# Two-block transformer kernel: one PSUM layout throughout, three plain indices per feed-forward layer, the second layer's parameters ordered late

## The chip, the cores and the metric

The kernel runs on one core of a Trainium2 chip. The metric is the device time of one execution in microseconds, the median of several runs. The engines are TensorE (PE, matmuls, with its weight loads shown as PEld), VectorE (DVE), ScalarE (ACT), GpSimd (POOL) and SyncE (SP), which issues all DMAs. Each engine has one queue of instructions and runs it strictly in order.

## The reference

Two transformer blocks follow each other, each with two layers, on 512 tokens of width 1024. The first puts 16 learned tokens in front (T = 528) and has in each layer a mixer (differential attention beside a gated recurrence) and a SwiGLU feed-forward part of inner width 2816. The change touches only this first block, above all the feed-forward part:

```python
for l in range(DEPTH):                      # DEPTH = 2
    hn = rms_norm(h, norm_mix_g[l])
    ...                                     # attention and recurrence, added to h
    hn = rms_norm(h, norm_ffn_g[l])
    g, u = jnp.split(hn @ w_gu[l], [D_FF], axis=-1)
    h = h + (jax.nn.silu(g) * u) @ w_down[l]
return h[:, N_META:, :]
```

The second block (convolution, two attentions, cross attention, squared-ReLU network) takes h as its input and is left as it is.

## The kernel before

All of it is float32. A product of two matrices is made of three matmuls with inputs that are split into a high and a low part (mm3, L105 to 108): the high part is a cast on ACT, the low part a subtraction on DVE, written by weight (L100, L102) for weights and by split (L200, L201) for the rest. The tensors stand with the feature on the partitions, in tiles of 128, and the tokens along the columns. Layer 0 computes all 528 columns in halves of 264, layer 1 only the 512 that are kept, in halves of 256.

**The feed-forward part** (FFN0 in layer 0, FFN1 in layer 1) goes through 22 indices; an index is one tile of 128 gate rows and one of 128 up rows (weight tiles t = 2i and 2i + 1). The first two indices are plain: early (L663 to 674) multiplies each weight tile with the normed input, 8 products of 128x128 on each half of the columns (24 matmuls a half), applies silu on ACT for a gate tile (L674) and multiplies with the up tile on DVE (L672). The input itself comes into being in that stretch, piece by piece (L682 to 696).

All other indices go through seven (L170 to 197), a scheme that makes the 2x2 block product out of seven block products (84 matmuls instead of 96). It needs sums of weight blocks: halves4 (L146 to 168) loads two weight tiles (wraw, wraw2) and lets POOL form ws (two operations, L155 and L156), a difference in place (L157) and ws4 (L158); then each is split on ACT and DVE. The results of the seven products (p1 to p7) are combined by DVE in a tile called quarters, after ACT has copied p1 to u (L186). ACT's silu (sl, L722) and POOL's gate product (L723) follow, and ACT and DVE split the result into yh and yl (L200, L201).

**The down projection** follows in five groups of 5, 5, 4, 4 and 4 indices (L728 to 744). A group has 8 tiles m of output rows; both halves of the columns stand in a pair of banks, and one DVE addition of all columns puts them into the residual h (hall, L743). Before a group starts, one index more than it needs is made, so seven-product indices come in runs of 4 (two plain ones ahead of them), 5, 4, 4 and 3.

**PSUM** has 8 banks. In the mixers and in block 2 they are handed out singly: three to mm, two to sc, one each to tr, av and bc. For a feed-forward part the pool is closed and another opened in which three pairs of banks (two) replace mm and sc; bank hands out the halves of a pair one after the other, so that the two parts of a pair are released together.

**What sets the order.** The program is written as loops; a scheduler turns it into one fixed list for each engine, by priorities that follow the order of writing. A buffer count (bufs) says how many tiles of one name may live at once; the next one waits until the last reader of the oldest is done. tc.issue_after puts what is made inside its scope behind a given instruction in the list. The small parameters of a layer (lt, gs and lc, L371 to 402, nearly all on DVE with 1 to 8 columns) depend on one DMA alone, so the scheduler puts those of layer 1 wherever it finds room.

## Time and profile before

| what | value |
|---|---|
| runs | 2880.06, 2882.56, 2883.85 us, median 2882.56 |
| the profiled execution | 2885.76 us, its span 2883.9 us, mean granted clock 0.982 |
| busy in the span | PE 2761.7 us (96%), DVE 1926.9 (67%), ACT 1323.9 (46%), POOL 719.8 (25%) |
| stages, us from the start | mixer 0 to 279, FFN0 to 665, mixer 1 to 909, FFN1 to 1288, block 2 to 2884 |

TensorE's clock as granted has two levels, 1.2 and 2.4 GHz, written as 0.5 and 1.0. In a table of busy times each stretch has the busy microseconds of each engine, with the number of instructions in brackets. In rows by time the first number is the start, the second the duration in us; what stands in square brackets is the time for which the engine idled before it and what released it. A name before the arrow is written, names behind it are read; the DVE pipeline lets the next instruction start a little before the last one's end.

### The profile page before, as it was taken

Reading aid. Unit: us, or ns where it says so; the run is one execution under the profiler, and the core shown is the slowest. Engines: PE = TensorE matmul, PEld = TensorE weight load, DVE = VectorE, ACT = ScalarE, POOL = GpSimd, SP = SyncE. Lnnn points to the kernel's source line nnn. Section 1 sums busy time; section 2 is a strip of 40 time slices with the busy share of each in tenths; the row PEclk is TensorE's granted clock in tenths of the full one; section 3 lists DMA queues with packets and bytes.
Section 4 is the critical chain, followed back from the end, with each engine's and each line's share of the span. In section 5 each row is a group of like instructions: output and inputs, shape, how many; then the busy total and the mean of one; then the engine's idle time right before and its main releaser. Section 6 shows DMA issues by size and latency. Waiting matters only on the chain.

```text
span 2883.9 us, 46217 instructions
## 1 busy us (share of the span) xinstructions
PE 2761.7 (96%) x17652; PEld 2467.3 (86%) x17652; DVE 1926.9 (67%) x3710; ACT 1323.9 (46%) x2366; POOL 719.8 (25%) x637
## 2 busy tenths in 40 slices
PE   8988899999998899999999999999999999999998
PEld 7888899999876899997789888888877898888887
DVE  7887866668888766668987563333689875633335
ACT  6664433436664433344675443332345754433323
POOL 0011644530112454433211031111322010311112
PEclk9999899999999999999999999999999999999999
DMA  4332133323332233335524213333255242133232
GB/s 146 88 79 92 47 102 94 99 78 119 87 82 84 73 101 100 104 97 142 144 74 134 72 59 108 96 95 95 76 140 145 67 134 79 59 102 95 95 96 66
DMA packets 101117, 277.41 MB, mean 96 GB/s; under 512 B 13856, under 2 KB 20512, under 8 KB 100896
## 3 DMA queue, kind: packets, MB, share of 16 engines
q1 hardware_dynamic: 100896, 274.45, 31.6%
q8 instruction: 140, 2.29, 0.3%
q14 instruction: 81, 0.66, 0.1%
HBM read 241.82 MB, written 2.10 MB: 85 GB/s over the span
## 4 chain that ended last, share of the span: by engine, by line
PE 78%; DVE 12%; issue 3%; POOL 3%; ACT 2%; DMA 1%; ACTq 0%; DVEq 0%; POOLq 0%; SPq 0%
PE mm L107 16%; PE mm L108 16%; PE mm L106 16%; PE two L108 6%; PE two L106 6%; PE two L107 6%; PE av L106 1%; PE av L107 1%; PE av L108 1%; DVE wlo L102 1%; PE av L240 1%; DVE wlo L201 1%; DVE sq L481 1%; PE av L851 1%; PE bc L966 1%
## 5 line engine op out<-in xcount | busy, mean ns | idle before, releaser
L100 ACT CAST whi<-wraw 128x1024 fp32r<-128x1024 f32 (+2 forms) x412 | 386.2, 941 | 627.5 <-PE mm L107 504.8
L106 PE MATMUL mm<-xh_all,whi 128*128 128x512 f32 (+2 forms) x1696 | 590.8, 351 | 15.0 <-ACT xh_all L339 7.1
L102 DVE TENSOR_TENSOR wlo<-wraw,whi 128x1024 fp32r<-128x1024 f32 (+2 forms) x389 | 458.2, 1179 | 209.5 <-ACT whi L100 208.4
L107 PE MATMUL mm<-xl_all,whi 128*128 128x512 f32 (+2 forms) x1696 | 593.9, 351 | 1.6 <-DVE xl_all L884 1.0
L108 PE MATMUL mm<-xh_all,wlo 128*128 128x512 f32 (+2 forms) x1696 | 590.0, 349 | 0.0
L106 PEld LDWEIGHTS mm<-xh_all,whi 128*128 128x128 f32 x1696 | 323.7, 192 | 53.2 <-ACT xh_all L339 7.1
L107 PEld LDWEIGHTS mm<-xl_all,whi 128*128 128x128 f32 x1696 | 324.4, 191 | 38.4 <-DVE xl_all L884 2.2
L108 PEld LDWEIGHTS mm<-xh_all,wlo 128*128 128x128 f32 x1696 | 325.3, 192 | 34.6
L1245 POOL TENSOR_TENSOR r<-r 128x512 f32<-128x512 f32 (+1 forms) x70 | 101.9, 1455 | 533.2 <-ACT r L1244 533.2
L106 PE MATMUL two<-yh,whi 128*128 128x264 f32 (+1 forms) x704 | 198.8, 283 | 1.8 <-ACT yh L200 1.8
L108 PE MATMUL two<-yh,wlo 128*128 128x264 f32 (+1 forms) x704 | 198.8, 283 | 0.0
L107 PE MATMUL two<-yl,whi 128*128 128x264 f32 (+1 forms) x704 | 198.4, 282 | 0.0
L106 PE MATMUL two<-xh_all,whi 128*128 128x264 f32 (+1 forms) x448 | 133.5, 301 | 18.4 <-DVE quarters L672 11.8
L812 DVE TENSOR_TENSOR hall<-hall,mm 128x512 f32<-128x512 f32 (+1 forms) x82 | 46.5, 567 | 146.0 <-PE mm L108 146.0
L107 PE MATMUL two<-xl_all,whi 128*128 128x264 f32 (+1 forms) x448 | 134.1, 300 | 4.1 <-DVE xl_all L689 4.1
L107 PE MATMUL two<-tl,whi 128*128 128x264 f32 (+1 forms) x480 | 136.2, 284 | 0.0
L108 PE MATMUL two<-th,wlo 128*128 128x264 f32 (+1 forms) x480 | 136.1, 283 | 0.0
L106 PE MATMUL two<-th,whi 128*128 128x264 f32 (+1 forms) x480 | 135.9, 283 | 0.0
L108 PE MATMUL two<-xh_all,wlo 128*128 128x264 f32 (+1 forms) x448 | 132.7, 297 | 2.2 <-DVE wlo L102 1.2
L106 PEld LDWEIGHTS two<-yh,whi 128*128 128x128 f32 x704 | 132.5, 188 | 2.2 <-ACT yh L200 2.2
L201 DVE TENSOR_TENSOR wlo<-wraw,whi 128x1024 fp32r<-128x1024 f32 x80 | 119.7, 1496 | 21.2 <-ACT whi L200 20.8
L107 PEld LDWEIGHTS two<-yl,whi 128*128 128x128 f32 x704 | 132.4, 188 | 0.1
(724 smaller groups left out, 7480.1 us busy)
## 6 DMA issues: line engine op xcount, KB each, us to landing
wraw<-w2f SPq DMA_DIRECT2D x128, 512.0 KB, 3.8
wraw<-w1gu SPq DMA_DIRECT2D x88, 512.0 KB, 3.6
wraw<-w2in SPq DMA_DIRECT2D x44, 512.0 KB, 3.8
wraw<-w1in SPq DMA_DIRECT2D x40, 512.0 KB, 3.6
wraw<-w2mkv SPq DMA_DIRECT2D x32, 512.0 KB, 3.6
wraw<-w1dn SPq DMA_DIRECT2D x48, 256.0 KB, 2.7
wraw<-w1dn SPq DMA_DIRECT2D x32, 320.0 KB, 2.9
wraw<-w1out SPq DMA_DIRECT2D x32, 256.0 KB, 2.7
```

Of the source, the lines that this page charges most:

```text
L100: nc.scalar.copy(hi[:, :kt], raw[:, :kt])
L102: (eng or nc.vector).tensor_sub(lo[:, :kt], raw[:, :kt], f(hi[:, :kt]))
L106: nc.tensor.matmul(ps, wh, xh, start=first, stop=False)
L107: nc.tensor.matmul(ps, wh, xl, start=False, stop=False)
L108: nc.tensor.matmul(ps, wl, xh, start=False, stop=last)
L201: nc.vector.tensor_sub(lo, x, f(hi))
L240: nc.tensor.matmul(ps[:ch, 2 * j:2 * j + 2], x[:, a + ch * j:a + ch * j + ch], rhs[:, :2], start=e == 0, stop=e == len(xs) - 1)
L481: nc.vector.tensor_mul(sq[:, a0:b0], sq[:, a0:b0], sin1[:, a0:b0])
L812: nc.vector.tensor_add(X(m, a, b), X(m, a, b), p)
L851: nc.tensor.matmul(ps[:, 4 * n + 2 * j:4 * n + 2 * j + 2], x[:, o:o + 128], one2, start=e == 0, stop=e == 1)
L966: nc.tensor.transpose(ps[:, 128 * j:128 * j + 128], p[:, 128 * j:128 * j + 128], ident)
L1245: nc.gpsimd.tensor_mul(r[:, a:b], r[:, a:b], r[:, a:b])
```

## The change

- One PSUM pool with the single banks stays open all the time. The pairs, and the closing and reopening around each feed-forward part, are gone.
- seven takes seven single banks, in the order tr, mm, sc, mm, sc, mm, sc for p1, p2, p6, p5, p7, p3, p4, and has seven DVE additions of one half of the columns.
- Three indices of each layer are plain instead of two (weight tiles t = 0 to 5), and quarters has three buffers in both layers.
- ws in halves4 has one buffer instead of two.
- The down projection uses proj: in layer 0 two halves with an addition each, in layer 1 one matmul of 512 columns for each weight, and one addition.
- The parameters of layer 1 are issued behind the addition for tile m = 0 of layer 0's last group.

```diff
-    def open_psum(name):
-        nonlocal psum, banks, paired, halves
-        paired, halves = name == "psum_f", None
-        banks.close()
-        banks = ExitStack()
-        psum = banks.enter_context(tc.tile_pool(name=name, bufs=1, space=bass.MemoryType.PSUM))
-
-    open_psum("psum")
+    psum = ctx.enter_context(tc.tile_pool(name="psum", bufs=1, space=bass.MemoryType.PSUM))
     EARLY = 4
     BANKS = {"mm": 3, "sc": 2, "tr": 1, "av": 1, "bc": 1}
...
-        s = pool.tile([128, 8, 128], F32, name="ws", bufs=2)
+        s = pool.tile([128, 8, 128], F32, name="ws", bufs=1)
...
-        p1 = bank("av")[:, :n]
-        p26, p57, p34 = (pair_of_banks()[:, :, :n] for _ in range(3))
+        p1, p2, p6, p5, p7, p3, p4 = (bank(t)[:, :n] for t in ("tr", "mm", "sc", "mm", "sc", "mm", "sc"))
         product(p1, a11, b11)
         nc.scalar.copy(u, p1)
-        product(p26[:, 0], a12, b21)
-        product(p26[:, 1], s2, t2)
-        nc.vector.tensor_add(e[:, 0:4:3], p26, twice(u))
-        product(p57[:, 0], s1, t1)
-        product(p57[:, 1], s3, t3)
-        nc.vector.tensor_add(e[:, 1:3], p57, twice(e[:, 3]))
-        nc.vector.tensor_add(e[:, 3], p57[:, 0], e[:, 2])
-        product(p34[:, 0], s4, b22)
-        product(p34[:, 1], a22, t4)
-        nc.vector.tensor_add(e[:, 1:3], p34, e[:, 1:3])
+        product(p2, a12, b21)
+        nc.vector.tensor_add(e[:, 0], p2, u)
+        product(p6, s2, t2)
+        nc.vector.tensor_add(e[:, 3], p6, u)
+        product(p5, s1, t1)
+        nc.vector.tensor_add(e[:, 1], p5, e[:, 3])
+        product(p7, s3, t3)
+        nc.vector.tensor_add(e[:, 2], p7, e[:, 3])
+        nc.vector.tensor_add(e[:, 3], p5, e[:, 2])
+        product(p3, s4, b22)
+        nc.vector.tensor_add(e[:, 1], p3, e[:, 1])
+        product(p4, a22, t4)
+        nc.vector.tensor_add(e[:, 2], p4, e[:, 2])
...
+            with ExitStack() as order:
+                if ended is not None:
+                    order.enter_context(tc.issue_after(ended.ins))
+
+                lt = small.tile([128, 8], F32)
...
-                firsts = [ff.tile([128, 4, half], F32, name="quarters", bufs=2 if l else 3) for _ in range(2)]
+                firsts = [ff.tile([128, 4, half], F32, name="quarters", bufs=3) for _ in range(3)]
...
-                    for t, n, j in ((0, n0, 0), (1, n0, 0), (2, n0, 0), (0, n1, 1), (1, n1, 1), (2, n1, 1), (3, n0, 0), (3, n1, 1)):
+                    for t, n, j in ((0, n0, 0), (1, n0, 0), (2, n0, 0), (0, n1, 1), (1, n1, 1), (2, n1, 1), *((t, n, j) for t in (3, 4, 5) for n, j in ((n0, 0), (n1, 1)))):
...
-                    if i < 2:
+                    if i < 3:
...
-                        e = seven(ff, w, rhs, half, 2 if l else 3)
+                        e = seven(ff, w, rhs, half, 3)
...
-                        ps = pair_of_banks()[:, :, :half]
-                        for j, n in enumerate((n0, n1)):
-                            for k, (yh, yl) in enumerate(ys):
-                                mm3(ps[:, j], w[0][:, k], w[1][:, k], yh[:, n], yl[:, n], k == 0, k == nf - 1)
-                        t = h[m][:, l0:].rearrange("p (a b) -> p a b", a=2)
-                        nc.vector.tensor_add(t, t, ps)
+                        for p, a, b in proj(w, ys, late):
+                            done = nc.vector.tensor_add(h[m][:, a:b], h[m][:, a:b], p)
+                            if f0 + nf == 22 and m == 0:
+                                ended = done
```

How the instructions stand on an engine follows from the scheduler, so three places are shown as they stand in its lists. Line numbers of the changed kernel are 8 to 24 lower: L651 is the former L672, L177 the former L201, L718 the former L743.

DVE at the front of FFN0, before: the last splits of the input (tl), then layer 1's parameters ahead of the product of a plain index.

```order
L201 TENSOR_TENSOR tl<-tt_3702,th 128x792
L371 TENSOR_TENSOR lt<-par 128x1
L372 TENSOR_TENSOR lt<-par 128x1
L381 TENSOR_SCALAR gs<-par 128x1
L382 TENSOR_SCALAR gs<-par 128x1
L383 TENSOR_SCALAR gs<-par 128x8
```

The same place after:

```order
L177 TENSOR_TENSOR tl<-tt_3699,th 128x792
L92 TENSOR_TENSOR wlo<-wraw,whi 128x1024
L651 TENSOR_TENSOR quarters<-quarters,mm 128x264
L92 TENSOR_TENSOR wlo<-wraw,whi 128x1024 x2
L651 TENSOR_TENSOR quarters<-quarters,mm 128x264
```

The product follows after one weight split; before, fifteen parameter operations stood between the two.

DVE at the end of FFN0, after: the additions of the last group, with the parameters between them; before, only additions, weight splits and the next norm's rows stood here.

```order
L718 TENSOR_TENSOR hall<-hall,mm 128x264 x2
L92 TENSOR_TENSOR wlo<-wraw,whi 128x512
L351 TENSOR_TENSOR lt<-par 128x1
L352 TENSOR_TENSOR lt<-par 128x1
L361 TENSOR_SCALAR gs<-par 128x1
L362 TENSOR_SCALAR gs<-par 128x1
L718 TENSOR_TENSOR hall<-hall,mm 128x264
L317 SCALAR_TENSOR_TENSOR xl_all<-hall,par,xh_all 128x528
```

Of the parameter operations 25 stand ahead of the last addition to the norm's sum (ss_acc).

ACT between two seven-product indices, before: silu of the finished one, the copy u of the next one's p1, then the cast yh of the finished one.

```order
L200 CAST whi_5193<-wraw2_5177 128x1024
L722 ACTIVATE sl_5168<-quarters_5073 128x528
L186 COPY u1_5202<-av_5203 128x264
L200 CAST yh2_5171<-quarters_5073 128x528
L200 CAST whi_5313<-wraw_5303 128x1024
```

The same place after:

```order
L701 ACTIVATE sl_5213<-quarters_5112 128x528
L176 CAST whi_5238<-wraw2_5222 128x1024
L176 CAST yh2_5216<-quarters_5112 128x528
L159 COPY u1_5247<-tr_5248 128x264
L176 CAST whi_5364<-wraw_5354 128x1024
```

The copy u and the cast yh have changed places, and the second weight's cast has come between silu and yh.

## Rows read from the trace of the kernel before

**Rows 1.** Window, length; busy (x) PE, PEld, DVE, ACT, POOL; PEclk, DMA share, GB/s

```profile
318.00:640.00 322.00, 321.82 (x2619) 321.39 (x2620) 222.47 (x271) 125.76 (x178) 150.04 (x92) 0.99 0.31 93
957.00:1265.00 308.00, 306.12 (x2560) 305.51 (x2559) 208.99 (x252) 125.01 (x178) 148.53 (x91) 0.99 0.31 94
```

**Rows 2.** TensorE's waits, FFN0 front (total us, times, longest).

```profile
PE two L106 <- DVE quarters L672: 8.0, 1, 8.0
```

**Rows 3.** TensorE's waits, FFN1 front.

```profile
PE two L106 <- DVE quarters L672: 3.8, 1, 3.8
...
PE two L106 <- ACT whi L100: 2.1, 1, 2.1
...
PE two L108 <- DVE wlo L102: 1.2, 1, 1.2
```

**Rows 4.** DVE in order of time, FFN0 front: start, duration, line, what.

```profile
309.72 1.22 DVE L371 TENSOR_TENSOR lt<-par 128x1 f32<-128x1 f32 x1
310.86 0.15 DVE L372 TENSOR_TENSOR lt<-par 128x1 f32<-128x1 f32 x1
...
317.58 0.43 DVE L672 TENSOR_TENSOR quarters<-quarters,two 128x264 f32<-128x264 f32 x1
```

**Rows 5.** Busy table in steps of 5 us, both fronts.

```profile
316.00:321.00 5.00, 2.94 (x13) 2.94 (x14) 4.79 (x12) 0.00 (x0) 1.04 (x1) 0.50 0.11 12
321.00:326.00 5.00, 5.00 (x35) 5.00 (x34) 3.56 (x8) 1.34 (x2) 1.28 (x1) 0.79 0.61 201
...
943.00:948.00 5.00, 5.00 (x24) 4.72 (x24) 1.32 (x3) 1.57 (x2) 5.00 (x4) 0.53 0.28 101
...
953.00:958.00 5.00, 2.39 (x11) 2.40 (x12) 4.18 (x8) 0.83 (x3) 0.00 (x0) 0.66 0.00 0
958.00:963.00 5.00, 5.00 (x32) 5.00 (x32) 3.10 (x7) 3.39 (x6) 0.00 (x0) 0.66 0.07 13
```

**Rows 6.** TensorE in order of time: 256 columns in FFN1, 512 in block 2.

```profile
1099.79 0.28 PE L107 MATMUL two<-yl,whi 128*128 128x256 f32 x1
...
1101.91 0.28 PE L107 MATMUL two<-yl,whi 128*128 128x256 f32 x1
...
1797.72 0.39 PE L106 MATMUL mm<-y0h,whi 128*128 128x512 f32 x1
...
1802.94 0.39 PE L108 MATMUL mm<-y7h,wlo 128*128 128x512 f32 x1
```

**Rows 7.** POOL in order of time, FFN0, weights of an index.

```profile
336.31 1.28 POOL L155 TENSOR_TENSOR ws<-wraw 128x512 f32<-128x512 f32 x1 [13.34 <-DMA wraw<-w1gu]
337.67 2.17 POOL L156 TENSOR_TENSOR ws<-ws,wraw 128x512 f32<-128x512 f32 x1
...
343.75 1.32 POOL L723 TENSOR_TENSOR quarters<-quarters,sl 128x528 f32<-128x528 f32 x1
346.30 1.34 POOL L155 TENSOR_TENSOR ws<-wraw 128x512 f32<-128x512 f32 x1 [1.23 <-DMA wraw<-w1gu]
```

**Rows 8.** DVE in order of time, same place.

```profile
345.77 0.71 DVE L201 TENSOR_TENSOR yl<-quarters,yh 128x528 fp32r<-128x528 f32 x1 [3.13 <-ACT yh L200]
...
349.26 1.70 DVE L201 TENSOR_TENSOR wlo<-ws,whi 128x1024 fp32r<-128x1024 f32 x1
...
358.02 1.23 DVE L201 TENSOR_TENSOR wlo<-wraw,whi 128x1024 fp32r<-128x1024 f32 x1 [0.24 <-ACT whi L200]
```

**Rows 9.** ACT in order of time, the cast behind the gate product.

```profile
414.58 0.63 ACT L200 CAST yh<-quarters 128x528 fp32r<-128x528 f32 x1 [2.69 <-POOL quarters L723]
```

**Rows 10.** DVE and TensorE, layer change, last addition to the norm's sum.

```profile
668.63 0.70 DVE L265 TENSOR_TENSOR ss_acc<-ss_acc,ss_sq 128x528 f32<-128x528 f32 x1
...
669.51 0.64 PE L240 MATMUL av<-one,ss_acc 128*88 128x2 f32 x7
```

**Rows 11.** TensorE, end of FFN1.

```profile
1289.03 0.36 PE L106 MATMUL mm<-xh_all,whi 128*128 128x256 f32 x1 [0.87 <-DVE hall L743]
```

More of the change, by code (lines that the diff above doesn't have):

```diff
@@ L108, in mm3 @@
         nc.tensor.matmul(ps, wl, xh, start=False, stop=last)
-    halves = None
     def bank(name):
-        nonlocal halves
-        if name == "mm" and paired:
-            if halves is None:
-                got = psum.tile([128, 2, 512], F32, name="two", bufs=3)
-                halves = got[:, 1]
-                return got[:, 0]
-            got, halves = halves, None
-            return got
         n = turns[name] = turns.get(name, 0) + 1
@@ L138, in proj @@
         return got
-    def twice(p):
-        return p[:, None, :].to_broadcast([128, 2, p.shape[1]])
-    def pair_of_banks():
-        return psum.tile([128, 2, 512], F32, name="two", bufs=3)
     def halves4(pool, w1, w2):
@@ L367, in both_blocks @@
                 nc.scalar.copy(rbc[:, a:b], p)
-            lt = small.tile([128, 8], F32)
-            nc.vector.tensor_mul(lt[:, 0:1], col(LAM), col(LAM + 1))
-            nc.vector.tensor_mul(lt[:, 1:2], col(LAM + 2), col(LAM + 3))
-            ps = bank("av")
-            nc.tensor.matmul(ps[:, :2], ones, lt[:, 0:2], start=True, stop=True)
-            nc.scalar.activation(lt[:, 2:4], ps[:, :2], AF.Exp, scale=float(D))
-            nc.vector.tensor_sub(lt[:, 4:5], lt[:, 3:4], lt[:, 2:3])
-            nc.vector.tensor_scalar(lt[:, 5:6], lt[:, 4:5], -lam_init, None, op0=OP.add)
@@ L398, in both_blocks @@
-            nc.vector.tensor_mul(lc[:, 4], lc[:, 4], lc[:, 2])
-            nc.vector.tensor_scalar(lc[:, 5], L, 0.0, None, op0=OP.min)
-            nc.vector.scalar_tensor_tensor(lc[:, 6], lc[:, 4], -2.0, lc[:, 5], op0=OP.mult, op1=OP.add)
-            nc.vector.tensor_scalar(lc[:, 7], lc[:, 6], 2.0, None, op0=OP.mult)
-            nc.vector.tensor_scalar(lc[:, 8], lc[:, 6], 4.0, None, op0=OP.mult)
+            with ExitStack() as order:
+                if ended is not None:
+                    order.enter_context(tc.issue_after(ended.ins))
+                lt = small.tile([128, 8], F32)
+                nc.vector.tensor_mul(lt[:, 0:1], col(LAM), col(LAM + 1))
+                nc.vector.tensor_mul(lt[:, 1:2], col(LAM + 2), col(LAM + 3))
+                ps = bank("av")
+                nc.tensor.matmul(ps[:, :2], ones, lt[:, 0:2], start=True, stop=True)
+                nc.scalar.activation(lt[:, 2:4], ps[:, :2], AF.Exp, scale=float(D))
+                nc.vector.tensor_sub(lt[:, 4:5], lt[:, 3:4], lt[:, 2:3])
+                nc.vector.tensor_scalar(lt[:, 5:6], lt[:, 4:5], -lam_init, None, op0=OP.add)
+                neglam = lt[:, 5:6]
+                gs = small.tile([128, 10], F32)
+                nc.vector.tensor_scalar(gs[:, 0:1], col(QG), 0.125, None, op0=OP.mult)
+                nc.vector.tensor_scalar(gs[:, 1:2], col(SUB), 1.0 - lam_init, None, op0=OP.mult)
+                nc.vector.tensor_scalar(gs[:, 2:10], par[:, BRG:BRG + 8], 0.5, None, op0=OP.mult)
+                lc = small.tile([128, 9, 4], F32)
+                L = par[:, LRU:LRU + 4]
+                nc.scalar.activation(lc[:, 0], L, AF.Abs)
+                nc.scalar.activation(lc[:, 1], lc[:, 0], AF.Exp, scale=-1.0)
+                nc.vector.tensor_scalar(lc[:, 2], lc[:, 1], 2.0, None, op0=OP.add)
+                nc.vector.reciprocal(lc[:, 2], lc[:, 2])
+                nc.vector.tensor_mul(lc[:, 2], lc[:, 2], lc[:, 1])
+                nc.vector.tensor_mul(lc[:, 3], lc[:, 2], lc[:, 2])
+                nc.vector.memset(lc[:, 4], 1.0 / 17.0)
+                for n in (15, 13, 11, 9, 7, 5, 3, 1):
+                    nc.vector.tensor_mul(lc[:, 4], lc[:, 4], lc[:, 3])
+                    nc.vector.tensor_scalar(lc[:, 4], lc[:, 4], 1.0 / n, None, op0=OP.add)
+                nc.vector.tensor_mul(lc[:, 4], lc[:, 4], lc[:, 2])
+                nc.vector.tensor_scalar(lc[:, 5], L, 0.0, None, op0=OP.min)
+                nc.vector.scalar_tensor_tensor(lc[:, 6], lc[:, 4], -2.0, lc[:, 5], op0=OP.mult, op1=OP.add)
+                nc.vector.tensor_scalar(lc[:, 7], lc[:, 6], 2.0, None, op0=OP.mult)
+                nc.vector.tensor_scalar(lc[:, 8], lc[:, 6], 4.0, None, op0=OP.mult)
@@ L775, in phase @@
             close(range(nm - tail, nm), w, xs, evac)
-    with banks, blk2:
+    with blk2:
         def parts(pool, name, shape=None, **kw):
```

32 lines of the change are left out of this document (7 added, 25 removed).

## The prediction

> **What bounds the kernel now.** I read the busy table by stage first, then the list of what TensorE waited for in each stage, then the rows around each long wait. In the first block's two feed-forward stages (FFN0 and FFN1) TensorE is the bound once the seven-product indices run: 321.82 us busy of 322, and 306.12 of 308 [rows 1]. A matmul of 264 columns takes 0.122 us there (321.82 us for 2619 recorded ones is 0.123, and a few records are missing). So a matmul saved is time gained and a new wait is time lost. Ahead of those stretches stands the costliest part. In FFN0 TensorE waits 8.0 us once, for the DVE product of a plain index at L672 [rows 2]. The rows show why: DVE ran the next layer's small parameter operations from 309.72 on, first of them 1.22 us long though it has one column, and reached L672 only at 317.58 [rows 4]. In FFN1 the same place waits 3.8 us, after two waits of 2.1 and 1.2 us for a weight's two casts [rows 3]. Behind each long wait the clock stands at its lower level for some microseconds: 35 matmuls in 5 us at a mean grant of 0.79, or 24 at 0.53 [rows 5], between the levels of 1.2 and 2.4 GHz.
>
> **The change, part by part.** Sums are against the profiled run, 2885.8 us (span 2883.9); the median of the runs shown is 3.2 us lower, and I carry the sum over to it.
>
> *The front of FFN0.* Gone is the 8.0 us wait, and for two reasons: the parameter operations leave this stretch, and the second half of the third weight tile no longer shares a pair of banks with the product that is late. The lower clock behind it goes too: 35 matmuls stand in 321 to 326 where 5 us hold 41, 0.7 us, and 13 ahead of them took 2.94 us instead of 1.6, 1.3 us [rows 5]. A third plain index takes 96 matmuls where a seven-product index takes 84: 12 x 0.122 = 1.5 us more. Together -8.6 us. Following the changed order through the stage row by row gives -9.2; I take -9, bounds -5 and -10.
>
> *The front of FFN1.* The 3.8 us go, with 11 matmuls in 2.39 us (1.1 lost) and 32 instead of 42 behind them (1.2 lost) [rows 5]. The 2.1 us wait is filled by the freed second half (24 matmuls, 2.8 us); the weight behind it is then about 1.4 us late, in place of the 2.1 and 1.2. Of what the lower clock took behind those two (24 matmuls where 42 fit, 2.2) I count 2.0 as gained. Against that stand 12 x 0.118 = 1.4 us of matmuls: 3.8 + 2.3 + 1.9 + 2.0 - 1.4 = 8.6. The row by row walk gives 9.7; I take -9, bounds -4 and -10, since DVE's margin at the sixth tile is under half a microsecond.
>
> *Down projection of layer 1.* 1056 matmuls of 256 columns become 528 of 512. Starts lie 0.118 and 0.227 us apart (18 steps in 2.12 us, 23 in 5.22) [rows 6]: 1056 x 0.118 - 528 x 0.227 = 124.6 - 119.9, so -4.7 us; I take -5. The Trainium skill (TensorE: Matmul & The Clock Gate, Back-to-back issue gap) gives N/2.4 ns and 2.5 ns on top; worked out, 109 and 216 ns, that would be an estimate of 1.4 us instead of 4.7, and the rows, being of this kernel, decide.
>
> *Parameters ordered late.* Thirty-one small DVE operations move to the end of FFN0. In the layer change the last addition into the norm's sum starts at 668.63 and TensorE takes it at 669.51 without a wait [rows 10], so DVE time added there is on the path. With POOL quiet such an operation takes 0.15 us [rows 4] and frees DVE in about half of that: some 25 ahead of the sum, 1.9 to 3.7 us; two additions of 264 for one of 528 (2 x 0.35 against 0.62, durations less the 0.08 us by which the next one overlaps) over seven tiles, 0.5 us; less a 1.15 us weight operation that now comes behind the sum, and about 1 us of gaps that absorb some. Net +2, bounds 0 and +5. At the end of FFN1 the 0.87 us that the pool switch costs [rows 11] may go: -0.5, bounds -0.9 and 0.
>
> *Seven products on single banks, one ws buffer.* For seven additions of one half, 0.43 us each like the product at L672 [rows 4], DVE has room: it is busy 222 us of 322 [rows 1]. The buffer is the part that costs. So far POOL's first addition (L155) starts the next index's weights as soon as the DMA lands: 346.30, while DVE is still to read the previous sum, 349.26 to 350.96 [rows 7, 8]. With one buffer it must wait for that read. Behind it on POOL stand three more additions and the gate product (L723), in order. Behind that product stand ACT's cast yh, and behind yh, in the changed order, ACT's copy of the next index's first product u, which so far went ahead of it; on DVE yl stands ahead of the additions that need u, and the next read of ws stands behind those. This is a closed loop, and I add it up.
> POOL's five operations took 336.31 to 345.07, 8.8 us [rows 7], the slow ones because each takes turns with a wide DVE operation; undisturbed they are 1.28 to 1.32 each, 6.4 us. With two instead of four DVE operations beside them: 7.7. Then yh 0.63, yl 0.71 [rows 8, 9] with u and the next cast beside it, the first addition 0.35, the low part of the first weight 1.23 (its cast adds 0.3), two additions 0.8, the read of ws 1.23: 5.1 with the hand-overs, as a wide operation frees DVE a little before its end. The loop takes 12.8 us for an index. TensorE needs 84 x 0.122 = 10.25, in layer 1 9.9. It notices at the last product, the third on the two sc banks: it must have the bank that DVE's second addition, inside the loop, gives back.
> So a seven-product index in the middle of a run loses 2.6 us (layer 1: 2.9). Runs are short, since the down projections between them let POOL catch up: per layer runs of 3, 5, 4, 4 and 3. Going through each run, its second index loses 0.6 to 1.9, the middle ones the full amount, the first and the last nothing. FFN0: 1.3 + (0.6 + 2.6 + 2.6) + 2 x (0.6 + 2.6) + 0.6 = 14.1. FFN1: 1.9 + (0.9 + 2.9 + 2.9) + (0.9 + 2.9) + (1.6 + 2.9) + 1.6 = 18.5, less the 1.9 us that this stretch waits already (308 less 306.12). In the down projections of FFN0 the three single banks and two additions for a tile cost another 2.0. Together +33. Bounds: with POOL undisturbed the loop is 11.5, and the losses are half, +17; with the 8.8 of the rows it is 13.9 and they are +43.
> Behind waits of 2.6 to 2.9 us the clock may fall as it does behind 3.8. Of eight such waits, two are followed by another wait that swallows the loss. I take +3, bounds 0 and +14.
>
> **Sum:** -9 - 9 - 5 + 2 - 0.5 + 33 + 3 = +14.5 us, 2900 for a run like the profiled one; on the median of 2882.6 it is **2897 us**.
>
> **The rivals.**
> *POOL is in time (faster).* If the gate product runs as soon as it may, u and the additions come in time and neither the buffer nor the queue behind it costs more than 5 us. It decides at the gate product: started within about 2.5 us of the end of the silu before it, the second addition still ends before the last product wants the bank, 6 x 1.46 = 8.8 us into the index. For it speaks that POOL's first additions so far start long before they are needed [rows 7]; against it that even undisturbed operations make the loop 11.5 where 10.25 is wanted. -21.5 + 5 = -16.5, so 2866.
> *The buffer costs nothing, the queue still does (no change).* Then u still stands behind yh and the gate product behind three additions, and the walk through the rows leaves about half the losses, +17 of 33: -4.5, so 2878, and up to 2888 with some clock lost.
> *The clock falls behind each wait (slower still).* The 3.8 us wait was followed by 2.3 us lost to the lower level [rows 5]; six of the eight long waits at that price make 14 instead of 3: 2908. The Trainium skill (TensorE: Matmul & The Clock Gate, A second HAM failure mode: psum-queue depth-cycling) says that turning through banks can make TensorE pause so often that its clock goes back and forth between its levels. No row here shows that yet: the two stretches stand at 0.99 [rows 1].
> *The change does not do what it says.* The order shows that the parameter operations do leave the front, so this could only be a front that waits as long for something else: 9 to 18 us of the gain are missing, and it ends near 2910.
>
> **How the numbers follow.** Forecast 0.50 (2888 to 2905), clock or front worse 0.20 (2905 to 2918), buffer free but queue not 0.17, POOL in time 0.13. The range that holds eight in ten leaves out most of the last and the end of the second: 2873 to 2916. A measurement of this kernel tells about 0.2%, 5.8 us, from no change, so faster is under 2876.8 and slower over 2888.3: faster 0.15, which takes in the lower end of the third case, the same 0.17, slower 0.68.
>
> **What the profile of the changed kernel would show.** Right: no wait of more than 2 us before the first seven-product index; in the middle of each run TensorE waiting 2 to 3 us before the last product, released by the second addition; POOL's first addition waiting for DVE's read of ws and not for a DMA; 12 to 13 us from one read of ws to the next; 512-wide matmuls 0.227 us apart; a wait of about 2 us at the first norm of layer 1. Wrong: seven-product indices 10.25 us apart throughout, or POOL still waiting for DMAs. The prediction falls if the loop takes under 11 us, or if the sc bank is given back before the last product needs it.

## The result, and the profile after

The changed kernel takes 2904.88 us, median of four runs (2902.96 to 2907.69), beside 2883.2 for the kernel before (one run more than in the table above): a ratio of 1.0077, 95% interval 1.006 to 1.0095, so 22 us slower. The forecast was 2897, slower, with 2873 to 2916 as its range. The profiled execution took 2905.03 us with a span of 2903.2, 19.3 more than before, where the sum had 14.5; the rest of the 22 us is that the profiled execution of before lay above its median.

The stages, each from TensorE's matmul on the norm's sum to the last matmul of the down projection, say where it went. FFN0 took 396.8 us instead of 385.2, FFN1 390.5 instead of 378.6; mixer 1 and block 2, which the change touches only at their starts, were 1.9 and 1.2 us shorter, the first mixer 1.2.

Busy times of the seven-product stretches after, in the columns of [rows 1]:

```profile
330.00:645.00 315.00, 299.93 (x2413) 297.21 (x2412) 208.33 (x320) 116.33 (x164) 130.49 (x87) 0.99 0.30 88
966.00:1270.00 304.00, 287.25 (x1930) 265.41 (x1930) 197.21 (x278) 111.81 (x160) 130.34 (x88) 0.98 0.31 90
```

TensorE had been busy for all but 0.2 and 1.9 us of such a stretch [rows 1]; now 15 and 17 us are idle. What it waited for, in FFN0 and then in FFN1 (total us, times, longest):

```profile
PE sc L96 <- DVE quarters L163: 13.6, 9, 2.5
PE mm L96 <- ACT yh L176: 1.4, 1, 1.4
PE mm L96 <- DVE hall L718: 1.3, 2, 0.7
...
PE sc L96 <- DVE quarters L163: 18.0, 9, 2.8
PE mm L96 <- ACT yh L176: 0.5, 1, 0.5
```

Nearly all of it is one wait: the last product p4 wants an sc bank (L96), and DVE's second addition (L163) has not given it back. The loop behind it can be read in one index in the middle of FFN0's run of five. Rows by time, POOL first, then ACT, DVE and TensorE:

```profile
413.12 1.29 POOL L129 TENSOR_TENSOR ws<-wraw 128x512 f32<-128x512 f32 x1 [5.30 <-DVE wlo L177]
...
419.55 1.32 POOL L702 TENSOR_TENSOR quarters<-quarters,sl 128x528 f32<-128x528 f32 x1
...
426.17 1.28 POOL L129 TENSOR_TENSOR ws<-wraw 128x512 f32<-128x512 f32 x1 [5.29 <-DVE wlo L177]
...
420.91 0.63 ACT L176 CAST yh<-quarters 128x528 fp32r<-128x528 f32 x1 [5.09 <-POOL quarters L702]
421.44 0.37 ACT L159 COPY u<-tr 128x264 f32<-128x264 f32 x1
...
421.57 0.71 DVE L177 TENSOR_TENSOR yl<-quarters,yh 128x528 fp32r<-128x528 f32 x1 [4.38 <-ACT yh L176]
422.20 0.43 DVE L161 TENSOR_TENSOR quarters<-mm,u 128x264 f32<-128x264 f32 x1
...
423.94 0.43 DVE L163 TENSOR_TENSOR quarters<-sc,u 128x264 f32<-128x264 f32 x1
...
424.82 1.22 DVE L177 TENSOR_TENSOR wlo<-ws,whi 128x1024 fp32r<-128x1024 f32 x1
...
424.42 0.59 PE L96 MATMUL sc<-th,whi 128*128 128x264 f32 x1 [2.54 <-DVE quarters L163]
424.81 0.42 PE L97 MATMUL sc<-tl,whi 128*128 128x264 f32 x1
425.02 0.42 PE L98 MATMUL sc<-th,wlo 128*128 128x264 f32 x1
```

POOL starts the weights at 413.12, released by DVE's read of ws and no longer by a DMA [rows 7]; its gate product ends at 420.87, 7.75 us later. yh follows, behind it the copy u, behind that DVE's two additions (with the low part of a weight between them), the second of which frees TensorE at 424.37, and then the next read of ws, to 426.04. POOL starts again at 426.17: 13.05 us for one turn.

The last two rows show a second cost. Starts are 0.21 us apart there instead of 0.122, at the lower level of the clock. In steps of 5 us, one place in FFN0 and one in FFN1 (columns as above, the granted clock is third from the end):

```profile
420.00:425.00 5.00, 2.46 (x18) 2.25 (x17) 3.15 (x6) 3.32 (x5) 0.87 (x1) 0.90 0.02 8
425.00:430.00 5.00, 5.00 (x34) 5.00 (x33) 4.41 (x7) 1.58 (x2) 3.75 (x3) 0.76 0.25 69
...
1070.00:1075.00 5.00, 3.52 (x30) 3.31 (x28) 1.37 (x3) 2.21 (x4) 2.75 (x3) 1.00 0.36 105
1075.00:1080.00 5.00, 3.73 (x19) 3.73 (x20) 4.86 (x9) 1.99 (x4) 1.28 (x1) 0.66 0.25 69
```

The wait of 2.7 us at 1060 left the clock at 1.00 (44 matmuls in 1065 to 1070); the next, at 1073, was followed by a grant of 0.66. Busy time times what the grant lacks of 1, summed over the 5 us steps of each stretch, makes 2.9 us in FFN0 and 5.5 in FFN1.

### The profile page after: what moved, and what is told of

The parts are those of the page before. It is cut to its first block, busy times and chain, and to the rows that moved or that the text cites. A ratio compares the mean times of both kernels' runs of the same rounds, so it can differ in the third digit from the quotient of the medians.

```text
span 2903.2 us, 45359 instructions
## 1 busy us (share of the span) xinstructions
PE 2767.8 (95%) x17148; PEld 2445.7 (84%) x17148; DVE 1924.7 (66%) x3856; ACT 1316.8 (45%) x2362; POOL 679.7 (23%) x627
## 4 chain that ended last, share of the span: by engine, by line
PE 57%; DVE 5%; issue 2%; ACT 2%; POOL 1%; ACTq 0%; POOLq 0%; DVEq 0%
PE mm L97 16%; PE mm L98 16%; PE mm L96 16%; PE sc L96 1%; PE sc L98 1%; PE sc L97 1%; DVE wlo L177 1%; PE av L96 1%; PE av L97 1%; PE av L98 1%; PE av L830 1%; PE bc L945 1%; PE tr L945 1%; DVE wlo L92 0%; ACT whi L176 0%
## 5 line engine op out<-in xcount | busy, mean ns | idle before, releaser
L96 PE MATMUL mm<-xh_all,whi 128*128 128x512 f32 (+2 forms) x2040 | 690.0, 341 | 18.9 <-ACT xh_all L316 8.1
L97 PE MATMUL mm<-xl_all,whi 128*128 128x512 f32 (+2 forms) x2040 | 694.3, 341 | 4.0 <-DVE xl_all L668 2.9
L98 PE MATMUL mm<-xh_all,wlo 128*128 128x512 f32 (+2 forms) x2040 | 688.4, 339 | 0.9 <-DVE wlo L92 0.8
L96 PEld LDWEIGHTS mm<-xh_all,whi 128*128 128x128 f32 x2040 | 390.5, 193 | 58.7 <-ACT xh_all L316 8.4
L96 PE MATMUL mm<-yh,whi 128*128 128x264 f32 (+1 forms) x528 | 169.7, 322 | 3.2 <-ACT yh L176 1.9
L97 PE MATMUL mm<-yl,whi 128*128 128x264 f32 (+1 forms) x528 | 169.9, 322 | 0.0
L98 PE MATMUL mm<-yh,wlo 128*128 128x264 f32 (+1 forms) x528 | 169.4, 321 | 0.0
L177 DVE TENSOR_TENSOR wlo<-wraw,whi 128x1024 fp32r<-128x1024 f32 x76 | 117.1, 1541 | 25.6 <-ACT whi L176 25.3
L96 PE MATMUL sc<-th,whi 128*128 128x264 f32 (+1 forms) x304 | 89.6, 295 | 31.7 <-DVE quarters L163 31.7
L96 PEld LDWEIGHTS mm<-yh,whi 128*128 128x128 f32 x528 | 99.0, 188 | 12.3 <-ACT yh L176 2.5
L97 PEld LDWEIGHTS mm<-yl,whi 128*128 128x128 f32 x528 | 99.2, 188 | 8.2 <-DVE yl L177 0.4
L98 PEld LDWEIGHTS mm<-yh,wlo 128*128 128x128 f32 x528 | 99.3, 188 | 8.0
L718 DVE TENSOR_TENSOR hall<-hall,mm 128x264 f32<-128x264 f32 (+1 forms) x120 | 61.1, 513 | 66.2 <-PE mm L98 65.9
L96 PEld LDWEIGHTS sc<-th,whi 128*128 128x128 f32 x304 | 58.7, 193 | 35.6 <-DVE quarters L163 35.4
```

Of the source, the lines that this page charges most:

```text
L96: nc.tensor.matmul(ps, wh, xh, start=first, stop=False)
L97: nc.tensor.matmul(ps, wh, xl, start=False, stop=False)
L98: nc.tensor.matmul(ps, wl, xh, start=False, stop=last)
L177: nc.vector.tensor_sub(lo, x, f(hi))
L718: done = nc.vector.tensor_add(h[m][:, a:b], h[m][:, a:b], p)
```

## Experiments

In the table a stage is counted as above, waits are TensorE's gaps of over 0.3 us from the first seven-product index to the end of the stage (those of a plain index left out), and the clock is the loss worked out as above for the same two stretches (the 3.0 us behind the wait of a plain index in FFN1 of the kernel before, and the 2.6 with the parameters late, are left out with those waits). Each kernel has one trace; medians are of 4 to 11 runs, and a ratio is to runs of the kernel before made beside them (medians 2882.2 to 2883.6). Where the steps of 5 us start moves the clock column by some 0.2.

| kernel | median us | FFN0, FFN1 | waits | clock |
|---|---|---|---|---|
| before | 2883.2 | 385.2, 378.6 | 0.9, 2.8 | 0 |
| changed | 2904.9 | 396.8, 390.5 | 16.4, 18.6 | 8.4 |
| ws twice in layer 0 | 2896.0 | 388.2, 385.7 | 10.0, 16.8 | 5.0 |
| p4 on av | 2888.0 | 390.6, 380.9 | 11.3, 9.8 | 3.0 |
| ws twice | 2884.3 | 384.5, 381.2 | 8.4, 9.4 | 2.8 |
| ws twice and p4 on av | 2871.4 | 382.0, 373.1 | 5.9, 3.9 | 0 |
| before with one ws | 2894.0 | 390.0, 382.6 | 6.2, 9.9 | 0 |
| before, parameters late | 2877.9 | 379.0, 377.9 | 0.9, 2.2 | 0 |
| before with both front edits | 2874.0 | 379.6, 375.5 | 0.9, 1.7 | 0 |
| changed, parameters free | 2902.9 | 397.7, 387.9 | 16.2, 16.9 | 7.6 |
| changed, two plain indices | 2919.5 | 404.7, 396.7 | 21.8, 23.2 | 11.5 |
| changed, down in halves | 2909.2 | 396.8, 392.6 | 16.5, 18.9 | 6.5 |
| pairs after the front | 2867.6 | 376.0, 370.1 | 0.9, 2.6 | 0 |

### Buffer and bank: a square of four

Two ws buffers in layer 0 alone:

```diff
-        s = pool.tile([128, 8, 128], F32, name="ws", bufs=1)
+        s = pool.tile([128, 8, 128], F32, name="ws", bufs=bufs)
...
-                            w = halves4(ff, w1gu[l, 2 * i], w1gu[l, 2 * i + 1])
+                            w = halves4(ff, w1gu[l, 2 * i], w1gu[l, 2 * i + 1], 1 if l else 2)
```

> The changed kernel with two ws buffers again in layer 0 (in layer 1 one stays). Loop theory: the single ws buffer closes the loop, so with two the two waits of 2.5 us in FFN0's run of five before the last product shrink to about 1 us or go; the idle time of TensorE in FFN0's seven-product and down stretch falls from 17 to about 9.5 us, the rest being single banks and the changed order of the queues; FFN1 stays as it is (waits of 2.7 us). Time 2904.9 - 7.5 = about 2897, FFN0 stage 389. Queue theory (the single banks and the copy u behind the cast yh cost it all, the buffer nothing): no change, 2905, waits of 2.5 us stay. Clock theory (most of the loss is the lower clock behind waits): FFN0 gains, but under 3 us, 2902 or more.

Measured: 2896.0 us, ratio to before 1.0042 (1.0029 to 1.0055), 9 less than the changed kernel. FFN0's waits fell from 16.4 to 10.0 and the stage by 8.7 us. FFN1's waits stayed at 2.7 us; that the stage is 4.8 us shorter in this profile comes from its clock and from one wait of 1.2 in place of 2.75. POOL's first addition no longer waits for DVE there, a DMA releases it, and in the run of five DVE's reads of ws follow each other after 11.8, 11.8 and 12.4 us instead of 13.05:

```profile
409.51 1.91 POOL L129 TENSOR_TENSOR ws<-wraw 128x512 f32<-128x512 f32 x1 [2.41 <-DMA wraw<-w1gu]
421.46 1.76 POOL L129 TENSOR_TENSOR ws<-wraw 128x512 f32<-128x512 f32 x1 [2.54 <-DMA wraw<-w1gu]
```

So the loop theory held in mechanism and size. Steps longer than TensorE's 10.25 us are left; what closes them is not shown.

The last product on another bank, one ws buffer:

```diff
-        p1, p2, p6, p5, p7, p3, p4 = (bank(t)[:, :n] for t in ("tr", "mm", "sc", "mm", "sc", "mm", "sc"))
+        p1, p2, p6, p5, p7, p3, p4 = (bank(t)[:, :n] for t in ("tr", "mm", "sc", "mm", "sc", "mm", "av"))
```

> The changed kernel with the last product p4 on the bank av instead of a third time on the two sc banks; ws keeps one buffer. Loop theory: the loop through ws runs on, so an index in the middle of a run still takes 12.8 us; only the place where TensorE notices moves, from the last product to the first products of the next index (waits of about 1.0 and 1.25 us for the low parts of its two weights). Only the ends of runs gain: idle 12.6 instead of 17.1 us in FFN0, 15.8 instead of 19.4 in FFN1 (down to about 16), together -5.6 us, and up to 4 more if the shorter waits no longer pull the clock down: 2895 to 2900. Bank theory (two sc banks for three products are the cause): the waits go and do not come back, 10.25 us for an index, -25 us, about 2880.

Measured: 2888.0, ratio 1.0019 (1.001 to 1.0028). The loop runs on as the loop theory says, 13.05 us from one start to the next:

```profile
412.49 1.29 POOL L129 TENSOR_TENSOR ws<-wraw 128x512 f32<-128x512 f32 x1 [5.30 <-DVE wlo L177]
425.54 1.29 POOL L129 TENSOR_TENSOR ws<-wraw 128x512 f32<-128x512 f32 x1 [5.30 <-DVE wlo L177]
```

But the gain was 17 us, not 5 to 10. FFN1's waits came out at 9.8 where 15.8 were expected: they are short ones (at most 1.2 us) at the weights of the next index, and behind these the clock fell less (3.0 instead of 8.4). So the loop theory had the mechanism, and neither theory had the size: the bank was worth more than the loop theory said and less than the bank theory.

Two ws buffers in both layers, with and without the other bank (u has one buffer, to make room):

```diff
-        s = pool.tile([128, 8, 128], F32, name="ws", bufs=1)
+        s = pool.tile([128, 8, 128], F32, name="ws", bufs=2)
...
-        u = pool.tile([128, n], F32, name="u1", bufs=2)
+        u = pool.tile([128, n], F32, name="u1", bufs=1)
```

> The changed kernel with two ws buffers in both layers (u with one buffer to make room), p4 still on the sc banks. It fills the square of buffer and bank: two buffers in layer 0 gave -9, p4 on av -17, both together -33.5. Additive theory (buffer and bank are two separate costs): -16.5, about 2888. Series theory (each wait hides behind the other, so that only both together free TensorE): -12 or less, 2893 or more. In layer 0 the steps between reads of ws should be 11.8 us again, not 13.0, in both theories, and the waits at the last product about 1 us instead of 2.5.

> The changed kernel with two ws buffers in both layers (u with one buffer to make room) and p4 on the bank av. Loop theory: with the loop open and TensorE not held at the last product either, idle time in the two stretches falls from 17 and 19 to about 8 and 9 us, what is left being waits of 0.5 to 1.3 us for the low part of the second weight and the additions of the down projection: 2904.9 - 18 = about 2887. If both the loop and the banks were harmless and the clock were the matter: above 2898. If single banks alone were at fault: the same as with p4 on av alone.

Measured: the buffer alone 2884.3, ratio 1.0002 (0.9993 to 1.001); both 2871.4, ratio 0.9958 (0.9946 to 0.9971). So -20.6 for the buffer, -17 for the bank and -33.5 for both. That is near the additive theory. The 4 us by which the two overlap are no finding, since the eleven runs with the buffer alone spread from 2876.8 to 2885.5. Counted beside p4 on av, the buffer is worth 16.6 us (2888.0 less 2871.4). With the buffer alone FFN1 keeps three waits of 1.9 to 2.1 us; with both edits no wait is left in the seven products that is longer than 1.3 us, and the clock stays up. What u with one buffer does was not run by itself. The changed kernel's fronts and down projection with these two edits beat the kernel before.

### One ws buffer in the old order

```diff
-        s = pool.tile([128, 8, 128], F32, name="ws", bufs=2)
+        s = pool.tile([128, 8, 128], F32, name="ws", bufs=1)
```

> The kernel before (pairs of banks, copy u ahead of the cast yh) with one ws buffer instead of two; nothing else of the change. If one ws buffer alone makes the loop of 13.0 us, whatever the banks and the order of the queues: some 1.5 us at each of the second and 2.8 at each middle index, +30, about 2912. If the loop is long because u stands behind yh and the additions behind yl (order of the queues that the single banks bring): in the old order u and the pair additions do not wait for the gate product, the loop is about 11 us, only waits of 0.5 to 1.2 us come, together +9: about 2892. If the buffer costs nothing in the old order: 2883.

Measured: 2894.0, ratio 1.0035 (1.0021 to 1.0049), 11 more than before. The turn is 12.5 us, longer than the 11 expected:

```profile
408.12 1.29 POOL L155 TENSOR_TENSOR ws<-wraw 128x512 f32<-128x512 f32 x1 [3.43 <-DVE wlo L201]
420.65 1.30 POOL L155 TENSOR_TENSOR ws<-wraw 128x512 f32<-128x512 f32 x1 [4.76 <-DVE wlo L201]
433.17 1.30 POOL L155 TENSOR_TENSOR ws<-wraw 128x512 f32<-128x512 f32 x1 [4.75 <-DVE wlo L201]
```

So the buffer alone closes the loop, and the old order takes only half a microsecond from it. Yet the buffer costs 11 us here and 20.6 in the changed kernel. TensorE notices at another place: here at the weights of a later index (waits of up to 1.1 us, 12 us more in all than before), in the changed kernel already at the index's own last product. That the place alone makes the difference is not shown: p4 on av, which moves the place and leaves the turn at 13.05 us, takes the buffer's price only from 20.6 to 16.6. The shorter turn, the order of the queues and the fewer additions come on top in the old order, unseparated.

### The fronts

The parameters free again in the changed kernel:

```diff
-                if ended is not None:
+                if False:
                     order.enter_context(tc.issue_after(ended.ins))
```

> The changed kernel without the order on the parameters of layer 1: they stand again in FFN0's front, between the products of the plain indices. If the parameters were the reason of the 8.0 us wait before: a wait comes back there, shorter than 8.0 since with single banks TensorE can go on for one or two halves of 2.9 us: 2 to 5 us, and 1 to 2 us of lower clock behind it: 2908 to 2912. If the freed second half and the third plain index did it alone: no wait, 2905. At the change of layers nothing should move (5.2 us in both kernels).

Measured: 2902.9, ratio 1.0067 (1.0055 to 1.008). No wait came back. DVE, in order of time:

```profile
312.43 0.42 DVE L651 TENSOR_TENSOR quarters<-quarters,mm 128x264 f32<-128x264 f32 x1
312.77 0.15 DVE L351 TENSOR_TENSOR lt<-par 128x1 f32<-128x1 f32 x1
...
317.23 1.25 DVE L376 TENSOR_TENSOR lc<-lc 128x4 f32<-128x4 f32 x1
...
321.49 0.42 DVE L651 TENSOR_TENSOR quarters<-quarters,mm 128x264 f32<-128x264 f32 x1
```

The second product comes 9 us behind the first, with the parameters between, as before the change; TensorE, with three single banks and more plain products to go on with, has no wait for a product of L651 in that front. The kernel is no slower for it either (2902.9 beside 2904.9): in the changed kernel the order on the parameters brings nothing that shows.

The parameters late in the kernel before, and both front edits there (parameters late, three plain indices, three buffers for quarters, one for u; the pairs stay). The first of these kernels has the pieces as far as `ended = done`, the second has all of them:

```diff
-            lt = small.tile([128, 8], F32)
...
+            with ExitStack() as order:
+                if ended is not None:
+                    order.enter_context(tc.issue_after(ended.ins))
+                lt = small.tile([128, 8], F32)
...
-                        nc.vector.tensor_add(t, t, ps)
+                        done = nc.vector.tensor_add(t, t, ps)
+                        if f0 + nf == 22 and m == 0:
+                            ended = done
...
-        u = pool.tile([128, n], F32, name="u1", bufs=2)
+        u = pool.tile([128, n], F32, name="u1", bufs=1)
...
-                firsts = [ff.tile([128, 4, half], F32, name="quarters", bufs=2 if l else 3) for _ in range(2)]
+                firsts = [ff.tile([128, 4, half], F32, name="quarters", bufs=3) for _ in range(3)]
...
-                    if i < 2:
+                    if i < 3:
```

> The kernel before with one part of the change: the parameters of layer 1 ordered late. If they alone make the 8.0 us wait in FFN0: it falls to about 2 us or less and with it 2 us of lower clock, and the layer change pays 0 to 2 us: 2883 - 8 = about 2875. If the pair of banks, whose second half is held by the late product, makes it: the wait stays over 5 us and the time within 2 us of 2883. FFN1 keeps its 3.8 us in both.

> The kernel before (pairs of banks, two ws buffers, copy u ahead of yh) with two parts of the change: three plain indices in both layers (u with one buffer to make room) and the parameters of layer 1 ordered late. If my split of the sum is right, the fronts bring the 7 to 9 us each that they brought in the changed kernel and the middle of the runs stays at 10.25 us without waits: 2883 - 14 + 0 to 2 at the change of layers = about 2870, faster than both kernels. If the freed banks were what made the fronts better, not the parameters and the third index (in pairs the second half of the third weight tile still shares its release with the late product): only half, about 2877. If single banks were needed for the third plain index: no gain, 2883.

Measured: 2877.9, ratio 0.998 (0.997 to 0.9989), and 2874.0, ratio 0.9972 (0.9962 to 0.9982). With the parameters late the 8.0 us wait [rows 2] became two (L676 is the former L672):

```profile
PE two L106 <- DVE quarters L676: 4.2, 2, 2.6
```

With the parameters late alone FFN0 is 6.1 us shorter. So the first of the two reasons that the prediction named for the 8.0 us removes most of it by itself. The second, the freed half of a pair, was run only together with the third plain index (the changed kernel with the parameters free). Together they remove all of it; what each does alone is open.

With both front edits, 2874 lies between the full gain (2870) and the half (2877). FFN0 is 5.6 and FFN1 3.1 us shorter than before, less than the fronts' 9.6 and 10.8 in the changed kernel. In pairs some waits stay, in FFN0 and then in FFN1:

```profile
PE two L106 <- DVE quarters L676: 1.8, 1, 1.8
...
PE two L106 <- ACT whi L100: 2.3, 1, 2.3
PE two L106 <- DVE quarters L676: 1.9, 1, 1.9
```

So in this layout the single banks are part of what the fronts gain.

Two plain indices in the changed kernel:

```diff
-                firsts = [ff.tile([128, 4, half], F32, name="quarters", bufs=3) for _ in range(3)]
+                firsts = [ff.tile([128, 4, half], F32, name="quarters", bufs=3) for _ in range(2)]
...
-                    if i < 3:
+                    if i < 2:
```

> The changed kernel with two plain indices a layer as before, so runs of 4, 5, 4, 4 and 3. If the third plain index is needed for the fronts: the waits of 8.0 and 3.8 us come back at least in part, 2910 or more. If the single banks alone keep TensorE busy there (as the run with the parameters in the front suggests): the fronts stay free of waits over 2 us, and what is left is one more seven-product index in each layer that costs the loop's 13.0 us instead of 11.7 and 11.3 for 96 matmuls: +3, 2908. If a shorter way to the first seven-product index were worth more than that: below 2902.

Measured: 2919.5, ratio 1.0126 (1.0109 to 1.0143), 15 more than the changed kernel. The fronts wait again, but at another place: the first seven-product index stands there before its weights do. TensorE in FFN1:

```profile
976.14 0.38 PE L96 MATMUL sc<-xh_all,whi 128*128 128x256 f32 x1 [3.73 <-ACT whi L176]
977.55 0.53 PE L98 MATMUL sc<-xh_all,wlo 128*128 128x256 f32 x1 [0.91 <-DVE wlo L177]
```

FFN0 has such a wait of 2.7 us. The third plain index is what covers the making of these weights, and with the loop it also replaces an index of 13.0 us by one of 11.7.

### Down projection in halves

```diff
-                        for p, a, b in proj(w, ys, late):
+                        for p, a, b in proj(w, ys, [(n.start, n.stop) for n in (n0, n1)]):
```

> The changed kernel with the down projection of layer 1 again in two halves of 256 columns (three single banks, two additions a tile). By the rows of block 2 (512 columns every 0.227 us) FFN1's down phases get 4.7 us longer: 2910. By the 0.234 us that the changed kernel shows in FFN1 itself: 1056 x 0.1185 - 528 x 0.234 = 1.6 us longer, plus up to 1 us where the two additions give a bank back late: 2906 to 2907.

Measured: 2909.2, ratio 1.009 (1.0075 to 1.0105). FFN1's five down phases, each from its first matmul to the start of the next one behind it, add up to 129.4 us, 5 more than the changed kernel's 124.45; with pairs, before, they took 126.0 without the pool switch. So 512 columns are worth 5 us in this layout and 1.5 against the kernel before. The size is that of the first case, the way is not. Spacing explains 1.6; most of the rest is that two additions give the single banks back late:

```profile
PE mm L96 <- DVE hall L718: 2.5, 4, 1.2
```

### A kernel made from this

The single banks stay through the front, and only then the pairs are opened; ws twice, u once, three plain indices, parameters late, layer 1's down projection in 512 columns on one bank of a pair. Against the kernel before with both front edits:

```diff
                 share("ff1")
-                open_psum("psum_f")
                 ff = ffn.enter_context(tc.tile_pool(name="ff", bufs=1))
...
                 made = []
+                open_psum("psum_f")
...
+                        if l == 1:
+                            ps = pair_of_banks()[:, 0, :2 * half]
```

> A kernel made from what the runs showed: the single banks stay through the front of each feed-forward part (three plain indices, parameters late), and only then the pairs open, with two ws buffers and the old order of the seven products; layer 1's down projection in matmuls of 512 columns. The front should then be as in the changed kernel with two ws buffers and p4 on av (about 4 us shorter in FFN0 and 6 in FFN1 than with pairs), the runs as in the kernel before with three plain indices (waits of under 1 us), and the down projection 1.4 us shorter: 2874 - 4 - 6 - 1.4 = about 2863. If the switch of the pools waits for the last front bank: up to 2 us a layer more, 2867. Slower than 2872 if the pairs cannot be had before the front's last product is read and DVE is late there.

Measured: 2867.6, ratio 0.9947 (0.9934 to 0.9959): 15 us faster than the kernel before, 37 than the changed one. With the single banks in front FFN0 is 3.6 and FFN1 5.4 us shorter than with both front edits in pairs, some 1.4 of the latter by the wide down projection; the expectation had 4, 6 and 1.4. The time is that of the second case, though TensorE waits only 0.6 us at the switch in each layer. Its seven-product stretches, and all that TensorE waited for from the first seven-product index of FFN0 to the start of mixer 1:

```profile
331.00:645.00 314.00, 312.86 (x2566) 312.67 (x2567) 213.26 (x259) 125.67 (x177) 140.72 (x88) 1.00 0.32 93
955.00:1260.00 305.00, 302.35 (x2075) 279.72 (x2076) 205.13 (x247) 122.94 (x175) 141.92 (x91) 1.00 0.32 95
```

```profile
PE mm L106 <- DVE hall L753: 1.1, 1, 1.1
PE two L106 <- ACT yh L200: 0.9, 1, 0.9
PE av L106 <- DVE quarters L675: 0.6, 1, 0.6
```

The last of these is the switch to the pairs (a plain index's product is still being read), the first the switch back behind FFN0.

## Why the prediction was right, step by step

| step | forecast | measured |
|---|---|---|
| front FFN0 | -9 | -9.6 |
| front FFN1 | -9 | -10.8 |
| seven products, one ws buffer | +33 | +36 |
| lower clock behind its waits | +3 | +8.4 |
| 512-wide down projection | -5 | -1.6 |
| parameters at the layer change | +2 | +0.1 |
| pool switch | -0.5 | -0.9 |
| the stages left alone | 0 | -3.4 |

The measured terms add up to 18 of the 19.3 us; the last is the two mixers and block 2 less the pool switch, and 2.9 of it is clock, by the same sum. The path (fronts gained, the loop lost) came out as forecast. That the total came so near owes something to luck: the terms missed upward by 11.8 us (seven products, clock, down projection) and downward by 8.1.

*The fronts.* From the norm's sum to the first seven-product index FFN0 took 47.0 us, with one half of a plain tile (2.9) still to come; now 50.6, with a plain index more. That is 0.7 us more for an index of 10.25 less, -9.6. For FFN1 the same count gives 47.3 before (40.7, the half of 2.8 and its wait of 3.8) and 49.4 after, so 2.1 less 9.95 and the 3.0 us that the clock lost behind that wait. No wait over 2 us stands in either front but the norm's own chain. The size was right, for the edits together. The runs do not split it into the prediction's two reasons: the late parameters take most of the 8.0 us away in the kernel before and bring nothing in the changed one, where the single banks and the third plain index are enough; and with pairs the same two front edits bring little more than half of it in FFN0 and less in FFN1.

*The loop.* Forecast 12.8 us a turn, of which POOL 7.7; measured 13.05 and 7.75. Middle indices were to wait 2.6 and 2.9 us, and do 2.54 and 2.72 to 2.76. The waits add up to 31.3 us more than before. Each also delays the matmuls that restart behind it; counted as what the distances between starts exceed the usual 0.122, 0.1185 and 0.234 us by, without the clock, it is about 36. The 2.0 us that the prediction set aside for FFN0's down projections are in this: they take 133.2 us instead of 130.5, each phase from its first matmul to the end of its last. The square of buffer and bank shows the mechanism and corrects one sentence: the buffer is not simply "the part that costs". It is worth 20.6 us, or 16.6 with p4 on av, the third use of the sc banks is worth 17, and in the old order the same buffer costs only 11. That the copy u behind yh lengthens the turn is seen only as the half microsecond between 12.5 and 13.05; no run changed it alone.

*The clock* was mis-sized: +3 forecast, 8.4 measured, inside the bounds of 0 to 14. The forecast let two of eight waits be swallowed and gave the rest half a microsecond each; the rows show six places where the clock falls, at 1.3 to 1.5 us each, while behind some waits as long it stays. The Trainium skill (TensorE: Matmul & The Clock Gate, A second HAM failure mode: psum-queue depth-cycling) says that pauses from turning through banks can send the clock back and forth. The trace agrees here, with grants of 0.66 to 0.91 in the 5 us steps behind some of the waits, where the kernel before lost nothing behind a wait of its seven products; without the waits (ws twice, p4 on av) they go.

*The 512-wide down projection* was mis-sized too. The step took its price from rows of block 2, 0.227 us [rows 6]. In the changed kernel's FFN1 the starts lie 0.233 us apart, six steps in 1.40:

```profile
1092.67 0.40 PE L96 MATMUL mm<-yh,whi 128*128 128x512 f32 x1
...
1094.07 0.40 PE L96 MATMUL mm<-yh,whi 128*128 128x512 f32 x1
```

1056 x 0.1185 - 528 x 0.234 = 1.6 us. The trace of the kernel before held the warning. Only the matmuls of block 2 that read y, those of [rows 6], stand 0.227 us apart; the larger group, which reads xh_all and xl_all, stands 0.232 apart. The next ones behind [rows 6] take 2.09 us for nine steps:

```profile
1805.25 0.40 PE L106 MATMUL mm<-xh_all,whi 128*128 128x512 f32 x1
...
1807.34 0.40 PE L106 MATMUL mm<-xh_all,whi 128*128 128x512 f32 x1
```

With 0.232 the term would have been -2.1. What makes the two groups differ is open. The estimate of 1.4 that the prediction worked out from the Trainium skill (TensorE: Matmul & The Clock Gate, Back-to-back issue gap) and set aside came nearest. That is luck: its 109 and 216 ns are both 8% short of the 118.5 and 234 measured here, and the two shortfalls cancel in the difference.

*The parameters* cost nothing at the layer change. DVE and TensorE there:

```profile
679.02 0.70 DVE L241 TENSOR_TENSOR ss_acc<-ss_acc,ss_sq 128x528 f32<-128x528 f32 x1
679.64 0.16 DVE L376 TENSOR_TENSOR lc<-lc 128x4 f32<-128x4 f32 x1
...
680.06 1.03 PE L216 MATMUL av<-one,ss_acc 128*88 128x2 f32 x12
```

From the last down matmul to TensorE's matmul on the sum it is 5.16 us, 5.10 before. Twenty-five operations stand ahead of the sum, as the order said (of 33; the prediction counted 31), but they found gaps on DVE. The step failed in counting them as work on the path; "gaps that absorb some" absorbed all. Its own terms also add up to only 0.3 to 2.1 us, of which it took the top.

*The pool switch:* the matmuls behind FFN1 start without the gap of 0.87 us [rows 11].

Of the rivals, "POOL in time" and "the buffer costs nothing" are refuted by POOL's rows and by the square. "The change does not do what it says" falls with the two fronts, which gained what was forecast. "The clock falls" was in part true, and with 5.4 us it is the largest of the misses. Two parts of the change were not run by themselves: the third quarters buffer of layer 1, and the copy u behind yh.

## What to carry to other kernels

Before a buffer count is lowered, follow the loop that it closes through every queue that it crosses, and compare one turn with the time of the engine that bounds: here 13.05 against 10.25 us. Ask also where that engine notices: the buffer cost 20.6 us where TensorE wanted a bank for its last product, 16.6 where it first wanted the next index's weights on the same turn, and 11 in the old order. A good part of a change (here the fronts and the wide down projection) can be taken alone: with the old seven products it made a kernel faster by half a per cent.

## What the runs showed of the hardware

The lower clock differs between executions by more than some of these effects. Of the eleven runs of the changed kernel with ws twice, those at a mean grant of 0.988 to 0.989 took 2876.8 to 2879.2 us, those at 0.983 to 0.985 took 2885.3 to 2885.5. Mixer 1 is the same code in all of these kernels; its granted clock was 0.99, 1.00, 0.97 and 0.97 in the kernel before, the changed one, before with both front edits, and before with the parameters late:

```profile
670.00:909.00 239.00, 225.35 (x1453) 193.87 (x1452) 202.66 (x492) 143.77 (x270) 28.42 (x42) 0.99 0.32 91
```

```profile
680.00:918.00 238.00, 224.72 (x1459) 192.79 (x1458) 204.00 (x499) 143.81 (x271) 28.39 (x42) 1.00 0.33 93
```

```profile
662.00:908.00 246.00, 233.62 (x1469) 200.56 (x1467) 202.11 (x512) 144.96 (x271) 29.28 (x42) 0.97 0.32 90
```

```profile
662.00:906.00 244.00, 231.65 (x1467) 198.96 (x1465) 202.33 (x511) 144.31 (x271) 29.27 (x42) 0.97 0.32 91
```

By the same sum as above these are 1.7, 0, 8.1 and 6.6 us. In block 2 the sum lies between 1.7 and 9.7 us over the thirteen traces. What makes the clock fall there more in one profile than in another is open; so an effect of a few microseconds is read from its own stage and from medians, not from two spans.
